# Whole-tile instead of half-tile instructions in a GELU-gated multiply whose transfers already fill the DMA engines

## The chip, the cores and the metric

One core of a Trainium2 chip; the program uses no other. The metric is device time in microseconds (us) of one execution, as the median of several runs. All runs quoted here are of the fast state, with a granted clock of 1.0. The span that the profile gives is some 1.7 us shorter than the run's time.

The input and the result lie in HBM, the memory of the device; a core computes on tiles in SBUF, its own on-chip memory. A DMA is a transfer between such memories, put into a queue by an engine and carried out, in packets, by 16 DMA engines; it "lands" when the engine that waits for it may go on.

## The reference

```python
# x: (32, 512, 2048) float32
half_dim = x.shape[-1] // 2
x1, x2 = x[..., :half_dim], x[..., half_dim:]
gelu_x1 = 0.5 * x1 * (1 + erf(x1 / np.sqrt(2)))
return (gelu_x1 * x2).astype(np.float32)
```

134 MB are read and 67 MB are written; each element of x1 gets one GELU and one multiply.

## The kernel before

The 16,384 rows are cut into 16 tiles. A tile has 128 partitions with eight consecutive rows each: 64 KB per partition in, 32 KB per partition out. There are two input tiles and two output tiles. Loads are issued on the SP queue, stores on the ACT queue (the last two tiles' on SP). ScalarE (ACT) computes the GELU in place, VectorE (DVE) the product, each in two steps of four rows.

```python
    R, STEP = 8, 4
    x_t = x_flat.rearrange("(n p r) d -> n p r d", p=P, r=R)
    o_t = out_flat.rearrange("(n p r) d -> n p r d", p=P, r=R)
    ...
    xpool = ctx.enter_context(tc.tile_pool(name="xpool", bufs=2))
    opool = ctx.enter_context(tc.tile_pool(name="opool", bufs=2))
    ...
    ahead = [load(0), load(1)]                 # on the SP queue
    for i in range(n_tiles):
        x_tile = ahead.pop(0)
        o_tile = opool.tile([P, R, half], out.dtype, name="o_tile")
        last = i == n_tiles - 1
        for r in range(0, R, STEP):
            rows = slice(r, r + STEP)
            nc.scalar.activation(
                out=x_tile[:, rows, :half], in_=x_tile[:, rows, :half], func=GELU
            )
            nc.vector.tensor_mul(
                out=o_tile[:, rows, :],
                in0=x_tile[:, rows, :half],
                in1=x_tile[:, rows, half:],
            )
            if last:
                store(nc.sync, i, o_tile, rows)
        if not last:
            store(nc.sync if i == n_tiles - 2 else nc.scalar, i, o_tile, slice(0, R))
        if i + 2 < n_tiles:
            ahead.append(load(i + 2))
```

The order in which one engine's instructions finally stand is not fixed by this text alone: the framework's scheduler chooses it when the kernel is built.

## Time and profile before

| | before |
|---|---|
| time, median | 471.43 us |
| span of the profiled run | 469.7 us |
| DVE busy, ACT busy | 140.2 us, 115.2 us |
| HBM traffic over the span | 429 GB/s |

The prediction shows the page's main lines and reads them. Two more views are needed. The first is the timeline of the ACT engine and its queue around tiles 3 and 4 (start, duration, instruction, and in brackets its idle time and what ended it); ACT lines are computation, ACTq lines are the issue of a DMA:

```profile
102.48 7.12 ACT L54 ACTIVATE x_tile<-x_tile 128x4096 f32<-128x4096 f32 x2 [21.79 <-DMA x_tile<-in_x_dram]
114.92 0.36 ACTq L45 DMA_DIRECT2D out_dram<-o_tile  x1
131.71 7.12 ACT L54 ACTIVATE x_tile<-x_tile 128x4096 f32<-128x4096 f32 x2 [22.10 <-DMA x_tile<-in_x_dram]
```

The store of tile 3 is issued at 114.92, between the GELUs of tile 3 and tile 4. The second is the end of the chain of waits:

```profile
405.29 44.00 DMA x_tile<-in_x_dram
449.29 0.02 issue
...
449.37 3.62 ACT x_tile L54
...
457.45 4.33 DVEq L93
```

The last load lands at 449.29; the first half of the last tile is ready for its store at 457.45.

### The profile page before, as it was taken

The page shows a single profiled execution, that of the slowest core. Times are in us where ns is not written, and L with a number is a line of the kernel's source. Part 1 is how long each engine was busy: PE and PEld are TensorE (multiplying, and loading weights), DVE is VectorE, ACT ScalarE, POOL GpSimd, SP SyncE. Part 2 cuts the span into 40 slices and gives each one's busy share as a digit, 9 for nine tenths or more (in the row PEclk, how much of TensorE's full clock was granted, in tenths as well). Part 3 has the DMA queues.
Part 4 walks back from the last instruction along what each step waited for, and adds up shares of the span by engine and source line. Part 5 has one row for each costly group of instructions (what it writes and reads, how often), then busy time and mean ns, then how long its engine had stood idle before and what let it go on. Part 6 is the DMA issues. An engine that isn't in the chain of part 4 may idle for free.

```text
span 469.7 us, 213 instructions
## 1 busy us (share of the span) xinstructions
DVE 140.2 (30%) x32; ACT 115.2 (25%) x33; POOL 0.2 (0%) x4
## 2 busy tenths in 40 slices
DVE  0070704307042070520606115060250702507043
ACT  1052306023060320603206041060500505005060
POOL 0000000000000000000000000000000000000000
DMA  8999999999999999999999999999999999999988
GB/s 357 446 446 357 446 446 446 402 446 458 391 446 444 433 463 402 435 413 491 402 419 430 491 402 402 446 491 402 402 446 480 413 402 444 449 446 402 474 375 357
DMA packets 4754, 201.35 MB, mean 429 GB/s; under 512 B 528, under 2 KB 528, under 8 KB 528
## 3 DMA queue, kind: packets, MB, share of 16 engines
q1 hardware_dynamic: 2736, 142.61, 70.5%
q10 hardware_dynamic: 2016, 58.72, 29.0%
q14 instruction: 2, 0.02, 0.0%
HBM read 134.22 MB, written 67.11 MB: 429 GB/s over the span
## 4 chain that ended last, share of the span: by engine, by line
DMA 77%; DVE 14%; ACT 6%; DVEq 1%; issue 0%; SPq 0%; ACTq 0%
DMA x_tile<-in_x_dram 77%; DVE o_tile L57 14%; ACT x_tile L54 6%; DVEq L93 1%; SPq L41 0%; ACTq L54 0%
## 5 line engine op out<-in xcount | busy, mean ns | idle before, releaser
L57 DVE TENSOR_TENSOR o_tile<-x_tile 128x4096 f32<-128x4096 f32 x32 | 140.2, 4422 | 321.6 <-ACT x_tile L54 321.6
L54 ACT ACTIVATE x_tile<-x_tile 128x4096 f32<-128x4096 f32 x32 | 114.0, 3608 | 340.5 <-DMA x_tile<-in_x_dram 340.5
L54 ACT ACT_TABLE_LOAD x1 | 1.3, 1283 | 0.7 <-PEq L82 0.7
L82 POOL MEMSET const-bfloat16-1.0<- 128x1 bf16 x1 | 0.1, 102 | 0.0
L82 POOL MEMSET const-uint8-127<- 128x1 uint8 x1 | 0.1, 101 | 0.0
L82 POOL MEMSET const-float32-0.0<- 128x1 f32 x1 | 0.1, 99 | 0.2 <-issue 0.2
L82 POOL MEMSET const-float32-1.0<- 128x1 f32 x1 | 0.1, 98 | 0.0
## 6 DMA issues: line engine op xcount, KB each, us to landing
out_dram<-o_tile ACTq DMA_DIRECT2D x14, 4096.0 KB, 41.8
out_dram<-o_tile SPq DMA_DIRECT2D x1, 4096.0 KB, 24.8
out_dram<-o_tile SPq DMA_DIRECT2D x2, 2048.0 KB, 6.9
x_tile<-in_x_dram SPq DMA_DIRECT2D x16, 45.5
```

The source lines that it names most:

```text
L54: nc.scalar.activation(out=x_tile[:, rows, :half], in_=x_tile[:, rows, :half], func=GELU)
L57: nc.vector.tensor_mul(out=o_tile[:, rows, :], in0=x_tile[:, rows, :half], in1=x_tile[:, rows, half:],)
L82: nc = _bacc.Bacc("TRN2", target_bir_lowering=False, num_devices=1)
L93: with _tile.TileContext(nc) as tc:
```

## The change

The intent is fewer, larger instructions: their fixed part is paid once per tile instead of twice. The last tile keeps its two steps, so that its first store can start early.

```diff
-    R, STEP = 8, 4
+    R = 8
...
-        for r in range(0, R, STEP):
-            rows = slice(r, r + STEP)
+        step = R // 2 if last else R
+        for r in range(0, R, step):
+            rows = slice(r, r + step)
```

The built instruction lists differ in one more thing, which no line of the diff names: on the ACT queue, the stores of tiles 3, 7 and 11 now stand behind the next tile's GELU (the list of the changed kernel, shortened):

```
Activation x_tile (tile 3)
Activation x_tile (tile 4)  [waits for tile 4's load]
DMACopy out<-o_tile (tile 3)
DMACopy out<-o_tile (tile 4)
Activation x_tile (tile 5)
```

## The prediction

> **What bounds the kernel now.** I read the page from the top: engine shares and slices, then the chain that ended last, the groups and the DMA issues; after that the chain in order of time, and a table of stretches.
>
> ```profile
> span 469.7 us, 213 instructions
> DVE 140.2 (30%) x32; ACT 115.2 (25%) x33; POOL 0.2 (0%) x4
> DMA  8999999999999999999999999999999999999988
> ...
> HBM read 134.22 MB, written 67.11 MB: 429 GB/s over the span
> ```
>
> No compute engine is busy a third of the time; the DMA engines are at 9 from the second slice on. The slices are rounded, so I asked for two-tile stretches (columns: length, busy time of DVE, ACT, POOL, granted clock, DMA share, GB/s):
>
> ```profile
> 2.00:36.00 34.00, 8.76 (x2) 7.13 (x3) 0.00 (x0) 1.00 0.96 412
> 36.00:44.00 8.00, 0.00 (x0) 0.00 (x0) 0.00 (x0) 1.00 1.04 393
> 44.00:102.00 58.00, 17.52 (x4) 14.25 (x4) 0.00 (x0) 1.00 1.00 434
> ...
> 276.00:334.00 58.00, 17.52 (x4) 14.24 (x4) 0.00 (x0) 1.00 1.00 434
> ...
> 449.00:458.00 9.00, 4.98 (x2) 7.12 (x2) 0.00 (x0) 1.00 0.95 409
> 458.00:468.00 10.00, 3.78 (x1) 0.00 (x0) 0.00 (x0) 1.00 0.99 419
> ```
>
> From 44 us to the last load the DMA share is 1.00 at 434 GB/s. A tile is 8.39 MB in and 4.19 MB out, 12.58 MB / 434 GB/s = 29.0 us, and 58.0 us for two is just the stretch. Everything: 201.33 MB / 434 = 463.9 us of the 469.7. The rest is head and tail.
>
> The chain of waits in order of time seems to say otherwise (start, duration, what):
>
> ```profile
> 276.46 3.62 ACT x_tile L54
> 280.09 0.02 issue
> 280.11 8.77 DVE o_tile L57 x2
> 288.88 0.02 issue
> 288.90 45.54 DMA x_tile<-in_x_dram
> 334.44 0.02 issue
> ```
>
> Here compute stands in line with a load: 3.62 + 8.77 + 45.54 = 57.9 us for two tiles. But a load of 8.39 MB at 434 GB/s needs 19.3 us, and a store moved beside it 9.7 us more; 45.5 us is mostly waiting in a queue behind the previous load. The compute in the chain is therefore not a cost by itself: ending it later shortens the queueing first.
>
> ```profile
> L57 DVE TENSOR_TENSOR o_tile<-x_tile 128x4096 f32<-128x4096 f32 x32 | 140.2, 4422 | 321.6 <-ACT x_tile L54 321.6
> L54 ACT ACTIVATE x_tile<-x_tile 128x4096 f32<-128x4096 f32 x32 | 114.0, 3608 | 340.5 <-DMA x_tile<-in_x_dram 340.5
> ...
> out_dram<-o_tile ACTq DMA_DIRECT2D x14, 4096.0 KB, 41.8
> out_dram<-o_tile SPq DMA_DIRECT2D x1, 4096.0 KB, 24.8
> ...
> x_tile<-in_x_dram SPq DMA_DIRECT2D x16, 45.5
> ```
>
> The first two lines give one instruction's duration and say that both engines idle for data. The others show that stores too are queued: 41.8 us from issue to landing against 9.7 us of bytes.
>
> **What the Trainium skill says.** "ScalarE: Activation LUTs", section "What ACT_TABLE_LOAD costs": an ACTIVATE with immediate scale and bias takes 186 ns + 0.833 ns per element of the row, and back-to-back ones overlap by about 93 ns. For 4,096 that is 3,598 ns (trace: 3,608), and two of them less the overlap 7.10 us (a tile's two take 7.12 in the trace): it agrees. "Perfetto Trace Analysis", section "Optimizing Scalar/DVE Operations", says that grouping helps if the engine is saturated, and that breaking instructions up may help where an unsaturated engine causes bubbles on another. These engines are not saturated, so the change goes in the direction that the page does not recommend, unless there are no bubbles to cause. "DMA: Bandwidth & Descriptors", section "Where 436 GB/s comes from", gives a ceiling of 435 GB/s; the trace runs at 434, so there is no headroom. The same page, "Queues, rings and completion order", says that each DMA engine alternates between the queues that have work, packet by packet. In the window from 220 to 335 us the load queue had 66.8% and the store queue 33.8% of the engines' time, in 572 and 576 packets: it agrees.
>
> **The change, part by part.**
>
> 1. Fewer instructions. Of fifteen tiles, each pair of ACTIVATEs (7.12 us) becomes one, by the page's rule 0.186 + 8,192 x 0.000833 = 7.01 us (estimate). A pair of multiplies takes 8.77 us; single ones 4,422 ns, so two overlap by 0.08 us, and the fixed part of an instruction is at least that: one of 8,192 should take 8.69 us (estimate: the pair less another 0.08). Saved: 15 x (0.11 + 0.08) = 2.9 us, all of it on idle engines: 0 us.
>
> 2. Lost overlap inside a tile. Now the multiply starts after half of the gelu. Landing to end of the multiplies is 276.38 to 288.88, 12.5 us. Afterwards it is 7.01 + 8.69 + about 0.13 of gaps = 15.8 us: the next load and the store are issued 3.3 us later, in fifteen tiles. What takes it up:
>  - Load: issued at 288.90, while the previous tile lands at about 305.5 (its gelu starts at 305.54). Until its bytes are through, some 2 us before the landing (estimate: the DMA share is 0.99 to 468 and the span ends at 469.7), the new load can't be served. Slack about 14.6 us, afterwards 11.3: 0 us.
>  - Store: each is in its queue for 41.8 us in a period of 29.0, so one is always in the queue ahead of it for about 12.8 us. 3.3 of them go: 0 us.
>  - Output buffer: the store issued at 288.90 lands at 330.7, and the multiply that reuses its buffer starts at 338.17. Slack 7.5 us, and the multiply moves later while the store's landing does not, so about 10.9: 0 us.
>
> 3. Order on the ACT queue. The built instruction lists of the two kernels show something that the diff does not tell: three stores (tiles 3, 7 and 11) now stand behind the next tile's gelu, which waits for that tile's load. Such a store is issued 29.0 us after its tile's landing and not at 12.5: 16.5 us later. The 12.8 us of backlog run out, so the store queue is empty for about 4 us. Meanwhile the next load is queued since 13 us and moves alone: the DMA stays full, loads get about 2 to 4 us ahead, the store some 4 to 7 us behind, and the buffer slack of 10.9 us still covers that. 0 us, less surely than point 2. Once stores lag, the next such store is late by less than its backlog, so the lag should not add up.
>
> 4. Tail. The last tile keeps its two halves: landing 449.3, then 3.62 + 4.43 = 8.1 us to the first half store, while the store of tile 14 fills the DMA until 458 (the row from 449 to 458 has a share of 0.95). In one step the half store would come at 449.3 + 15.8 = 465, some 7 us of empty DMA; this is why the change splits it. As built, 0 us, or up to 3.5 us if store 13 lags at the end and holds back the last multiply.
>
> 5. Head. The first tile's store and the third load are issued at 38.5 instead of 35.1. The second load's bytes end at about 44.4 - 2 = 42.4, so 3.9 us remain. The first load took about 1 us from issue (0.73) to the first bytes. That fits, but it is the smallest slack of all, and the row from 36 to 44 with 393 GB/s is already a little below 434 (0.8 us lost). Expected cost 0 to 3.4 us, I take 0.3.
>
> Sum: 0 + 0 + 0 + 0.1 + 0.3 = +0.4 us, so 471.8 us.
>
> **The rivals.**
>
> - The chain at face value. Each pass of two tiles would grow by 3.3 us, eight passes: +27 us, about 498 us. For it speaks the chain, in which every link holds ACT and DVE; against it the share of 1.00 and the 14.6 us of slack.
> - The late stores leave holes. If the DMA queues do not cover each other, each of three late stores costs up to the 4 us in which the store queue is empty, and with 3.5 us at the tail the time is 471.4 + 12 + 3.5 = about 487 us. For it: stores really are moved by 16.5 us. Against it: the load queue has work then.
> - Head only: +3.4 us, 474.8 us, if the first store and third load come too late.
> - Fewer fixed costs pay: -2.9 us, 468.5 us. Against it: those engines wait 321.6 and 340.5 us for data. At most 469.7 - 463.9 = 5.8 us lie outside full-rate transfer, and much of that is the first and the last latency.
>
> **Range and chances.** All the main terms are zero because slack covers them; errors go mostly up: the head (up to 3.4) and the tail (up to 3.5) together make 475 with half of both. Below 470.8 the DMA has almost nothing to give. Range 470.8 to 475.5. Over 2% faster would be under 462 us, less than the bytes take at 434 GB/s: 0.01. Over 2% slower is above 480.9 and needs holes in the steady part: 0.05. Within 2%: 0.94.
>
> **What would show it.** In the profile after: DVE x17 with about 8.7 us per whole tile, ACT about 7.0 us; in the stretches between 44 and 440 us a DMA share of 1.00 and 434 GB/s (steps 2 and 3); a load's time from issue to landing shorter by about 3.3 us, near 42 us, in the chain; a store's near 38 us; the three late stores issued after their next tile's landing; the multiply never waiting for a store. Wrong if: stretches at tiles 3 to 5, 7 to 9 or 11 to 13 fall below 434 GB/s; the row from 36 to 44 us falls by over 10%; the row after the last landing shows an empty DMA; or the chain has the same 45 us in its loads beside a longer compute.

## The result, and the profile after

The changed kernel takes 478.18 us in the median of four runs (477.95 to 478.5), against 471.43. Ratios here are the mean time of one kernel's fast runs over that of the other's fast runs of the same rounds, so not quite the ratio of the medians: it is 1.0142, with a 95% interval of 1.0127 to 1.0157. The loss is small, but clear.

The page of the changed kernel, its first lines:

```profile
span 476.7 us, 182 instructions
DVE 139.1 (29%) x17; ACT 113.8 (24%) x18; POOL 0.2 (0%) x4
DMA  8999999999999999999999999999999999999977
...
HBM read 134.22 MB, written 67.11 MB: 422 GB/s over the span
```

The busy times fell a little, as the larger instructions promise; the DMA row is full as before, except for the last two slices. By stretches (the same columns as in the prediction):

```profile
44.00:102.00 58.00, 17.39 (x2) 12.79 (x3) 0.00 (x0) 1.00 1.00 434
...
160.00:218.00 58.00, 17.39 (x2) 12.34 (x2) 0.00 (x0) 1.00 1.01 431
218.00:276.00 58.00, 17.38 (x2) 14.06 (x2) 0.00 (x0) 1.00 0.99 422
276.00:334.00 58.00, 17.39 (x2) 14.06 (x2) 0.00 (x0) 1.00 1.00 429
...
449.00:458.00 9.00, 0.00 (x0) 2.60 (x1) 0.00 (x0) 1.00 0.98 422
458.00:468.00 10.00, 8.76 (x2) 4.52 (x2) 0.00 (x0) 1.00 0.65 275
468.00:478.00 10.00, 0.00 (x0) 0.00 (x0) 0.00 (x0) 1.00 0.64 270
```

Two things are to be seen. First, up to 160 us nothing is lost; from there to 392 us the DMA share stays about 1.00 and yet the engines move only 422 to 431 GB/s. They are as busy as before and do less in the same time: single packets take longer. Second, at the end (458 to 478 us) the share is 0.65: a part of the DMA engines has nothing to do. Before, that share was 0.99 from 458 to 468 us, and the program was over at 469.7.

The end of the chain of waits after:

```profile
412.19 43.13 DMA x_tile<-in_x_dram
455.32 0.02 issue
...
455.40 3.62 ACT x_tile L55
...
463.47 4.34 DVEq L94
```

The last load lands at 455.32 instead of 449.29, 6.0 us later. From there to the end it is 21.4 us against 20.4: 1.0 us more. Together these are the 7.0 us between the spans.

The timeline of ACT around tiles 3 and 4 after:

```profile
101.21 7.03 ACT L55 ACTIVATE x_tile<-x_tile 128x8192 f32<-128x8192 f32 x1 [21.98 <-DMA x_tile<-in_x_dram]
130.21 7.03 ACT L55 ACTIVATE x_tile<-x_tile 128x8192 f32<-128x8192 f32 x1 [21.97 <-DMA x_tile<-in_x_dram]
130.23 16.12 ACTq L45 DMA_DIRECT2D out_dram<-o_tile  x2
```

The store of tile 3 is issued at 130.23, right after the GELU of tile 4 could start, and not at about 117 us, when its own product was ready. This is the late store. It is issued once tile 4 has landed; the GELU itself needs not to have finished. (The line's x2 takes in the next issue too, that of tile 4's store, which ends at 146.35.)

The profile's views give averages over the 16 DMA engines. The trace also records each packet, and each engine's end marker for each DMA (a 4-byte packet). The records name no engine; the packets of one engine are found by stringing them together, each beginning where another ends. From those, the time in us of the first and of the last of the 16 engines to finish a DMA, and the distance:

```
                 before                     after
load of tile 4   130.47 .. 130.97 (0.50)    129.15 .. 129.76 (0.62)
load of tile 8   246.47 .. 246.97 (0.50)    244.74 .. 247.71 (2.97)
load of tile 11  333.47 .. 333.97 (0.50)    331.20 .. 336.89 (5.68)
load of tile 15  448.26 .. 448.88 (0.62)    446.03 .. 454.95 (8.92)
store of tile 14 457.94 .. 458.79 (0.85)    459.34 .. 465.85 (6.51)
last store       468.15 .. 468.51 (0.36)    474.18 .. 475.57 (1.40)
```

Before, the engines go in step from beginning to end. After, they keep step until the late store at 130 us and drift apart from the load of tile 6 on. The fastest engine finishes the last load 2.2 us earlier than before, the slowest 6.1 us later, and a load has landed when the slowest has finished. Each engine has a fixed share of every DMA (eight packets of each load and each whole-tile store), so nobody takes over the rest: while the slowest still works on tile 14's store, the fastest wait for the last tile. The slowest engine ends tile 14's store 7.06 us later than before, and that is the loss. Followed through the records, the two slowest engines' load packets are longer than 2.418 us by 7.4 us in sum, about 1.4 us on the fastest. The distances in the table are not lengthening alone: an engine that serves one more store packet (1.213 us) before its last load packet ends that load as much later.

### The profile page after: what moved, and what is told of

Read it like the earlier page. It is cut to its first block, busy times and chain, and to the rows that moved or that the text cites. A ratio compares the mean times of both kernels' runs of the same rounds, so it can differ in the third digit from the quotient of the medians.

```text
span 476.7 us, 182 instructions
## 1 busy us (share of the span) xinstructions
DVE 139.1 (29%) x17; ACT 113.8 (24%) x18; POOL 0.2 (0%) x4
## 4 chain that ended last, share of the span: by engine, by line
DMA 72%; DVE 14%; ACT 11%; DVEq 1%; issue 0%; SPq 0%; ACTq 0%
DMA x_tile<-in_x_dram 72%; DVE o_tile L58 14%; ACT x_tile L55 11%; DVEq L94 1%; SPq L41 0%; ACTq L55 0%
## 5 line engine op out<-in xcount | busy, mean ns | idle before, releaser
L58 DVE TENSOR_TENSOR o_tile<-x_tile 128x8192 f32<-128x8192 f32 (+1 forms) x17 | 139.1, 8190 | 328.7 <-ACT x_tile L55 328.7
L55 ACT ACTIVATE x_tile<-x_tile 128x8192 f32<-128x8192 f32 (+1 forms) x17 | 112.6, 6627 | 348.0 <-DMA x_tile<-in_x_dram 348.0
```

Source lines behind the costliest of these rows:

```text
L55: nc.scalar.activation(out=x_tile[:, rows, :half], in_=x_tile[:, rows, :half], func=GELU)
L58: nc.vector.tensor_mul(out=o_tile[:, rows, :], in0=x_tile[:, rows, :half], in1=x_tile[:, rows, half:],)
```

## The experiments

The theory (A): the whole-tile instructions cost nothing; the three stores that the build moved behind the next GELU change the order in which load and store packets alternate on the DMA engines, and in the new order load packets take longer. The first rival (B): the later issue (3.3 us in fifteen tiles) or the long instructions themselves do it. Where a kernel needs a fixed order on the ACT queue, it has a helper that adds an order-only edge between two instructions:

```python
    def behind(later, earlier):
        if earlier is not None:
            tc.add_manual_dep(later.ins, earlier.ins.name, no_sync, reason="queue order")
```

All timed runs are over three rounds beside the kernel before on the same chip. Its median was 471.63 us in the first group of four, 471.68 in the second, and 471.39 and 471.56 beside the last two.

### Whole tiles with the stores in order

```diff
+            behind(gelu, stored)        # the previous tile's store on the ACT queue
```

> The changed kernel with one thing undone: on the ACT queue every gelu is kept behind the store of the tile before it, so that no store is issued late. Theory A (the three late stores, tiles 3, 7 and 11, upset the alternation of the two DMA queues): 471.4 us within 0.7, a full load packet takes 2.42 us throughout, the last load lands near 449 us. Rival B (whole-tile instructions themselves, 3.3 us later issue in fifteen tiles, cost the time): 478 us within 1, as the changed kernel.

Measured: 471.27 us, ratio 0.9986 (0.9972 to 1.0001). Two of its stretches:

```profile
218.00:276.00 58.00, 17.38 (x2) 14.07 (x3) 0.00 (x0) 1.00 1.00 434
...
458.00:468.00 10.00, 3.78 (x1) 0.00 (x0) 0.00 (x0) 1.00 0.99 419
```

The rate and the end are those of the kernel before. No load packet after 60 us takes over 2.418 us, and the engines are 0.53 us apart at the last load. The instructions are the changed kernel's, the issue of loads and stores is as late as in it (the store of tile 3 at 117.15 us); only the order is restored. So B falls, and the whole loss belongs to the order.

### Half tiles with the late stores

```diff
+    LATE = (3, 7, 11)
...
+        if held is not None:            # the store of the tile before, behind this gelu
+            late_store = store(nc.scalar, i - 1, held, slice(0, R))
+            behind(late_store, gelu)
```

> The kernel before, with its half-tile instructions, but the stores of tiles 3, 7 and 11 put behind the next tile's gelu on the ACT queue. Theory A: 478 us within 1.5, load packets longer than 2.42 us after the first late store, the last load landing near 455 us. Rival B: 471.4 us within 0.7.

Measured: 477.58 us, ratio 1.0123 (1.0108 to 1.0139).

```profile
218.00:276.00 58.00, 17.52 (x4) 13.24 (x4) 0.00 (x0) 1.00 0.99 422
...
458.00:468.00 10.00, 8.76 (x2) 3.88 (x2) 0.00 (x0) 1.00 0.89 378
```

The late stores alone, with the old instructions, bring the loss: the same 422 GB/s, and the last load lands near 454.7 us. With the first run this settles which part of the change acts. One side effect belongs to this kernel alone: in its view of waits, 207.7 us in ten waits of DVE end with a store's landing (the multiplies wait until their output tile is free), where the changed kernel has 328.7 us, all ending with ACT. So these waits are not needed for the loss, which the changed kernel has without them. In this kernel too the DMA share stays at 0.99 to 1.01 from 44 to 449 us, and 13.0% of the load packets take over 2.5 us.

### The same order, with the compute on one partition

Wrong result. Each GELU and multiply works on one partition of 128 and takes as long as before.

```diff
-                out=x_tile[:, rows, :half], in_=x_tile[:, rows, :half], func=GELU
+                out=x_tile[:1, rows, :half], in_=x_tile[:1, rows, :half], func=GELU
```

(the multiply likewise; the two output tiles are filled with zeros at the start).

> Wrong result on purpose. The changed kernel with its late stores, but each gelu and multiply works on one of 128 partitions: the same durations, 1/128 of the SBUF traffic of the compute engines. Theory A in the form A1 (the DMA queues and memory alone make the packets longer): 478 us within 1.5 with long packets. Form A2 (long packets come from ACT and DVE accesses meeting the loads in SBUF once the order is upset): 471.4 to 473 us, packets at 2.42 us.

Measured: 478.27 us, ratio 1.0137 (1.0122 to 1.0152), the engines 8.8 us apart at the last load. This run was made because many of the long packets fall into the time in which ACT works, which looked like a collision in SBUF (80% of them start while ACT computes, against 29% of all load packets). With 1/128 of the compute engines' traffic the loss is the same: A1 holds, the compute engines' accesses are not the cause.

### All transfers in one queue

```diff
-            store(nc.sync if i == n_tiles - 2 else nc.scalar, i, o_tile, slice(0, R))
+            store(nc.sync, i, o_tile, slice(0, R))
```

> The changed kernel with all stores on the SP queue, in one line with the loads, so that no two DMA queues alternate and the ACT queue has no stores. Theory A: 471.4 us within 1, as nothing is upset; packets at 2.42 us. Rival B: 478 us within 1.5, as the whole-tile instructions are kept.

Measured: 474.86 us, ratio 1.0069 (1.0051 to 1.0087). A miss for both: it is half of the loss. Without alternation each engine moves eight load packets, then eight store packets, and so on. Some load packets are longer here too (3.8% of them over 2.5 us), the engines are 4.4 us apart at the last load, and the end shows it:

```profile
458.00:468.00 10.00, 7.08 (x2) 1.79 (x1) 0.00 (x0) 1.00 0.77 326
```

So "the alternation of two queues is upset" is too narrow. A reading that fits is that the sequence matters in which an engine meets loads and stores, and that a single queue has a sequence that is not the best one either; this run alone does not show it.

### One late store, early or near the end

```diff
-    LATE = (3, 7, 11)
+    LATE = (3,)          # the second kernel: (11,)
```

> The changed kernel with queue order kept for all stores but one: only the store of tile 3 is behind the next gelu. Theory A-once (one late store moves the two DMA queues into an alternation that then stays and lengthens load packets in every later tile): about 477 us, 5 us or more over the kernel before, the packet lengths growing from 160 us to the end. Theory A-each (every late store costs its own share and the queues recover): 473.6 us, a third of the loss.

> As the run before, but only the store of tile 11 is late. A-once: the alternation is bad for 4 tiles instead of 12, so a loss of about a third, 473 to 474.5 us. A-each: 473.6 us too; this run separates nothing alone, but with the run before it does: A-once wants the early one to cost two to three times as much as this one, A-each the same.

Measured: with tile 3 alone late, 477.94 us, ratio 1.0131 (1.0114 to 1.0147); with tile 11 alone, 472.98 us, ratio 1.0027 (1.0007 to 1.0048). In the first, the rate never comes back:

```profile
276.00:334.00 58.00, 17.39 (x2) 14.06 (x2) 0.00 (x0) 1.00 0.99 420
```

One late store is enough. It moves the store queue against the load queue, the new sequence repeats in every later tile, and the engines drift for the rest of the kernel. The early one costs 6.3 us, the late one 1.3: A-once is right in its direction, though I had expected a ratio of two to three and not of five. (That ratio is not firm: the four executions of the second kernel lie between 471.79 and 473.84 us.) I had also expected the packets to grow longer towards the end, and they did not: from 160 us on each stretch has about a fifth of its load packets over 2.5 us. The second kernel's engines are 2.5 us apart at the last load, the first one's 4.3. The changed kernel loses about as much as the first one with engines 8.9 us apart: the distance shows that something drifts, but it does not measure the loss. The lengthening on the slowest engine comes nearer (7.4 us in both).

The sequences can be read from the packet records (one engine; start in us, what, duration in us):

```
before                         after
149.97 load   2.418            153.62 load   2.418
152.39 store  1.213            156.04 store  1.213
153.60 load   2.418            157.25 store  1.213
156.02 load   2.418            158.46 load   2.418
158.43 store  1.213            160.88 load   2.418
159.65 store  1.213            163.30 store  1.213
160.85 load   2.418            164.51 load   2.594
163.27 store  1.213            167.10 store  1.213
```

Where one DMA ends and the next begins in a queue, the other queue gets two packets in a row. Before, two loads come first and then two stores; after, two stores and then two loads, and the first long packet in this engine is the third load, at 164.51 (on other engines already the second of the pair, from 160.65 on). With the stores in order and issued 3.3 us later, load and store alternate strictly and there are no pairs at all.

A count over all engines of the changed kernel (from 150 to 445 us) bears this out within one run. Where the two loads follow the two stores directly, about 20% of 743 load packets take over 2.5 us; where a load and a store stand between the two pairs, about 5% of 321. It also tells where the engines come to differ, and why the later late stores may add nothing to the loss: after the late store of tile 7 about half of the engines pass into the second sequence, and after that of tile 11 all but two are out of the first. These two are the slowest at the end. With tile 3 alone late, none passes. In the half-tile kernel the contrast is weaker (19% of 952 against 12% of 168), so the place of these pairs is not the whole of it.

### Other output addresses

Wrong result: tile i is written to the place of tile i + 5.

```diff
-        return queue.dma_start(out=o_t[i][:, rows, :], ...
+        return queue.dma_start(out=o_t[(i + 5) % n_tiles][:, rows, :], ...
```

> Wrong result on purpose. The changed kernel, three late stores, but every tile is written five tiles further on in the output, so that the HBM addresses written while a load runs are others. If the longer packets come from the order of packets alone: 478 us within 1. If they come from particular pairs of addresses in HBM: different by over 2 us, in either direction.

Measured: 478.41 us, ratio 1.0145 (1.013 to 1.016), the engines 9.4 us apart at the last load. Particular pairs of HBM addresses are not the cause.

### Reads in place of the stores

Wrong result on purpose.

```diff
+        if i < n_tiles - 2:
+            flat = o_tile.rearrange("p (a b) d -> p a (b d)", b=2)
+            return queue.dma_start(out=flat, in_=x_t[i][:, : R // 2, :])
```

> Wrong result on purpose. The changed kernel, three late issues, but each store of tiles 0 to 13 is replaced by a read of as many bytes, in packets of the same size, on the same queue, at the same moment, from the input into the output tile; only the last two tiles are written. If the longer packets need reads and writes of HBM to mix: all full packets at 2.42 us, no drift of the DMA engines, 471.4 us within 1.5. If the order of the two queues alone does it: 477 us or more and long packets.

Measured: 470.94 us, ratio 0.9987 (0.9972 to 1.0002). The packet records show the same sequence as the changed kernel, with two 32 KB packets and then two of 64 KB in nearly every tile; the mean load packet is 2.421 us and none is over 2.465. The engines are 1.7 us apart from tile 5 on, and stay so to the last load. The sequence alone does no harm; it matters what the second queue's packets move.

### What of a store it is: two more

A store reads SBUF and writes HBM. One kernel replaces it by a copy from HBM to HBM at the same moment, the other by a copy from the output tile in SBUF onto itself. Both give a wrong result.

```diff
+        if i >= n_tiles - 2:
...
+        flat = o_t[i].rearrange("p (a b) d -> p a (b d)", b=2)
+        copy = queue.dma_start(out=flat, in_=x_t[i][:, : R // 2, :])
+        tc.add_manual_dep(copy.ins, muls[i].ins.name, sync, reason="same moment")
```

> Wrong result on purpose. The changed kernel with its three late issues, but each store of tiles 0 to 13 is a copy of as many bytes from the input in HBM to the same place of the output in HBM, issued at the same moment (it waits for the same multiply). So HBM is written as in the changed kernel, and SBUF is not read by the stores. If writes to HBM between the loads' reads are what lengthens the load packets: long load packets after 160 us and a drift of the DMA engines, 476 us or more. If reads of SBUF by the stores are needed for it: load packets at 2.42 us, 471.4 us within 1.5. If the copies themselves are slower than stores were, the run tells nothing.

```diff
+        if i < n_tiles - 2:
+            return queue.dma_start(out=o_tile[:, rows, :], in_=o_tile[:, rows, :])
```

> Wrong result on purpose. The changed kernel with its three late issues, but each store of tiles 0 to 13 reads its output tile in SBUF, as a store does, and writes the same bytes back to the same place in SBUF instead of to HBM. If reads of SBUF by the store queue beside the loads are enough to lengthen load packets: long packets after 160 us and a drift, 476 us or more. If it takes both, the reads of SBUF and the writes to HBM: packets at 2.42 us and 471.4 us within 1.5. If a copy inside SBUF is itself slower than a store was (its packets over 1.21 us each), the run tells nothing of the time, and only the load packets count.

Measured: the copies in HBM take 471.61 us, ratio 1.0003 (0.9987 to 1.002), and the engines do not drift after tile 5 (2.4 us apart from there to the last load, the length of two 32 KB packets). The copies in SBUF take 486.11 us, ratio 1.0286; their own packets were longer from the start (about 1.65 us up to 140 us), so its time says nothing, as foreseen. Its load packets do: after 160 us some are long and the engines drift, from 2.4 us apart at tile 5 to 6.2 at the last load, with no store to HBM in that time. The load packets (64 KB) of all runs, from the packet records:

```
                                mean us,     share over 2.5 us,
                                160 to 448   60 to 448 us
before                          2.418        0.1%
after                           2.459        10.4%
whole tiles, in order           2.418        0.0%
half tiles, late stores         2.481        13.0%
one partition, late             2.455        9.6%
one queue                       2.431        3.8%
late at tile 3 only             2.482        14.6%
late at tile 11 only            2.428        2.9%
other output addresses          2.458        9.7%
reads for stores                2.421        0.0%
HBM to HBM for stores           2.419        0.6%
SBUF onto itself for stores     2.429        3.1%
```

This points to the reading of SBUF by the second queue beside the loads, rather than to the writing of HBM. The HBM copies came into a slightly different sequence on most engines (a load, a store and then two loads after the two stores), but not on all: where they had the changed kernel's own sequence, none of 280 load packets takes over 2.5 us. With the copies in SBUF it is about 9% of 443 in that sequence and 0.3% of 635 in the other. So in this sequence neither writing HBM (these copies) nor writing SBUF (the reads above) lengthens the loads. That reading SBUF alone does is not shown: the copies in SBUF also write SBUF and slow themselves, and no run has a second queue that only reads it. Why two stores before two loads lengthen load packets, and two loads before two stores do not, stays open.

No version came out that beats both kernels. The best, whole tiles with the stores in order, equals the kernel before within the interval. That was to be expected where bytes alone take 463.9 of 469.7 us.

## Why the prediction was wrong

The prediction was 471.8 us with a range of 470.8 to 475.5; 478.18 was measured. By its steps:

1. Fewer instructions: right. A whole-tile GELU takes 7.03 us (7.01 predicted), a multiply 8.69 us (8.69), and the saving on idle engines is worth nothing.
2. Later issue: right in what it costs. Landing to issue is 15.8 us as predicted, and the kernel with the stores in order shows that it costs 0 us; its loads take 42.1 us from issue to landing, as predicted. One detail was wrong: a store's time to landing was to fall to 38 us and is 42.3 there. The first store, issued 3.3 us later, enters the alternation behind a load packet instead of before it, and with it all that follow. It did not matter, because the output tile still had room. One reading was off: a load's last bytes come about 0.4 us before its landing (448.88 and 449.29 us), not 2 us; the load's slack was larger than stated.
3. Order on the ACT queue: this is the step that failed, at "the DMA stays full ... 0 us". The premises were right: three late stores, issued with the next tile's landing, the load queue ahead (tile 5's load ends 2.4 us earlier than before), the store queue behind (tile 3's store ends 4.8 us later), and no multiply that waits for a store (in the view of waits, DVE waits for ACT alone). The conclusion was not. A full DMA was taken to be a DMA at 434 GB/s. The share did stay at 1.00, but packets became longer, one engine more than the other, and 7.4 us of lengthening on the slowest engine put its end 7.06 us later. That was the time lost. I had also argued from the lag of stores that such events do not add up. A single event suffices, and its effect goes on.
4. Tail: the idle DMA that it allowed for came (a share of 0.65), but not for its reason. It was to come if the store of tile 13 held back the last multiply; it came because the load of the last tile lands with the slowest engine.
5. Head: right. Issue at 38.40 us (38.5 predicted), and the stretch from 36 to 44 us has 393 GB/s before and after.

The rival "the late stores leave holes" named the right culprit and a wrong mechanism, with 487 us against 478. There are no holes in the steady part. My own test for error ("stretches ... fall below 434 GB/s") is what showed it.

Of the Trainium skill, the prediction used the ceiling of 435 GB/s ("DMA: Bandwidth & Descriptors", section "Where 436 GB/s comes from"), and the trace with its 434 agrees. The same section sets a lower limit, about 358 GB/s, for transfers between HBM and SBUF; the 434 GB/s here, on one core, are such transfers, so that limit did not hold.

## What to carry to other kernels

Where several DMA engines split every transfer evenly, the slowest of them sets the time: look at the rate beside the busy share, at how long single packets take and at how far apart the engines finish, before you call a full DMA a constant. A change of instruction sizes can change the built order of a queue that also issues DMAs. Compare the built lists, and pin the order with an order-only edge if it matters; here that was worth 7 us. And when slack hides a delay, ask not only whether the resource has other work then, but in which sequence it will do the work afterwards.

## What the Trainium skill lacked or had wrong

- "DMA: Bandwidth & Descriptors", section "Queues, rings and completion order": packet-wise alternation holds in the records. It lacks that the sequence that comes out of it changes how long packets take: 64 KB load packets at 2.418 us in one sequence of loads and stores, 2.459 to 2.482 us in the mean in another, and 2.421 us if reads stand in for the stores.
- "Perfetto Trace Analysis", section "What “DMA-bound” means", names specific DMA engines as a possible bound. That section lacks how they come to differ under even shares and a busy share of 1.00: 0.6 us apart at the last load before, 8.9 us after. Which of the 16 were the slow ones, the kept records do not say.
- "SBUF — State Buffer", section "SBUF: two separate sides", says that DMA and compute accesses cannot slow one another. The runs agree: with 1/128 of the compute traffic the time was 478.27 us, as with all of it. On the DMA side the section allows for contention where several DMA engines write; of one engine's loads beside its stores it says nothing. The copies from SBUF onto themselves (1.65 us per 32 KB packet beside loads up to 140 us, 1.22 after 160, against 1.213 for stores) suggest that these two can slow each other.
- No page has it: when the first store joins a running load, the load packet then under way takes 0.7 to 1.3 us longer (3.14 to 3.76 us on the 16 engines before), not so when the second queue's packets come from HBM (2.445 us in the mean where reads stand in for the stores, 2.418 where copies in HBM do).
